# Moving dependent DMA issues from the SyncE queue to the GpSimd queue, and one weight split behind a normalisation, in a two-layer GDN / attention / FFN kernel

## The chip, the cores and the metric

One core of one Trainium2 chip runs the whole program. Time is device microseconds (us) of one execution; several executions are timed and their median is the kernel's time. One further execution is taken by the hardware profiler, and every trace row below is from that one. Engine names are those of the profile: PE is the matrix engine (PEld its weight loads), DVE, ACT and POOL are VectorE, ScalarE and GpSimd, SP is SyncE, which here only issues DMAs. A name with a q behind it (SPq, POOLq) is an engine's instruction queue; it runs its instructions in the order that the program gives them, so an issue that waits holds up every issue behind it.

## The reference

The reference computes a two-layer backbone on 256 latent tokens and 256 context tokens of width 2048, all in float32. Layer 0 is a mixer of 8 bidirectional gated-DeltaNet heads (a chunked linear recurrence that needs the inverse of a triangular matrix for every chunk, head and direction) beside 8 neighbourhood-attention heads; layer 1 is a gated short convolution. Each layer is modulated by factors computed from a conditioning vector and is followed by a SwiGLU FFN of hidden width 5632. In short:

```
for l in range(2):
    shifts, scales, gates = split(silu(c) @ ada_w[l] + ada_b[l])
    h = rmsnorm(x) * g * (1 + scale) + shift
    y = even_mixer(h, hc, ...) if l == 0 else shortconv_mixer(h, ...)
    x = x + gate1 * y
    x = x + gate2 * swiglu(rmsnorm(x) * g' * (1 + scale') + shift')
return rmsnorm(x)
# inside even_mixer, per head, direction and chunk of 64 tokens:
t_inv = inverse(eye + strict_lower(kb @ k.T * decay))
u, w  = t_inv @ (v * beta), t_inv @ (kb * exp(gc))
S     = S * exp(g_last) + k_dec.T @ (u - w @ S)
```

## The kernel before, in words

**Weights.** Every matrix product streams its weight from HBM in pieces of 128 x 1024 (`raw`, 512 KB, loaded on SP's queue by `load_w`, line 235). `split_w` makes two parts of each piece, a rounded `whi` (ACT, line 175) and a remainder `wlo` (DVE, line 249), and three matmuls (activation high by `whi`, high by `wlo`, low by `whi`) stand for one float32 product. `fm_stream` (line 347) holds the weight still, `tm_stream` (lines 302, 303, 307 and, for the last group, 319) holds the activation still. In layer 0's mixer there are four `raw` buffers and three of each split; later six of each.

**The order of the work.** The code only emits instructions. A scheduler at build time orders them per engine, by readiness on its own timeline and by the order of emission; `issue_after(i)` queues an instruction behind `i` on `i`'s engine (and only there), `follow` does so for one pair. While the projections stream, a plan keyed by stream steps (`P_CH`, `P_INV`) emits the stages of the GDN part, so that they interleave with the projections; `ada_mixer` adds the loads (`araw`, line 435) and sums (`acc`, line 441) of the modulation factors.

**The GDN stages.** `chunk_matrices(seq)` runs for the context (seq 1) and then for the latents (seq 0, `own_chunks`). For each group of four heads (q) and each token tile it makes the matrices `nt` (DVE, line 994), whose diagonal 32 x 32 blocks go to `dgs`, whose 32-wide off-diagonal blocks go to `n32` (POOL copies, line 1013) and whose 64-wide ones go to `n64`; `n64` and `n32` are stored to DRAM (lines 1020 and 1021, shown as `nd<-n`), the diagonal blocks go out to `dl` and come back as `lsol` (lines 1023, 1027), are inverted by substitution on DVE (lines 1036 and 1038) and stored as `dz` (line 1045). `load_diag` clears `xd` and `xdT` (POOL, lines 1060 and 1061) and reads `dz` back with 8 DMAs (line 1066) per sequence and q: 32 rows by 16 blocks by 32 floats each. There are two buffers of `xdT` and one of each `xd`. `inverses` (matmuls at lines 1092, 1099, 1105) builds the whole inverse from them, and `scan` runs the recurrence over it. `scan` loads keys as `ktok` and values as `vtok` (`load_tok`, line 956); for seq 1 and q 1 the keys go to the buffer of `lsol`, the source of one of the `dz` stores. All of these DMAs are issued by SP. POOL issues seven DMAs of its own, the reload `hC<-h_d` (line 1284).

**Evacuation of the value projection.** `stage` copies a finished PSUM bank to one of three buffers `nst` (`copy`, lines 170 and 172, in turn on ACT and DVE) and SP stores it (line 1260, `kb_d<-nst` and `vb_d<-nst`).

**Normed streams.** Three streams begin right behind a residual sum and take its RMSNorm as input: the gate projection of the FFN of layer 0, the convolution's input projection, and the gate projection of the FFN of layer 1. `Lead.scale` normalises the first 512 columns of the first token tile on DVE (line 1427, kept as `xi`) behind the sum of squares (line 1418) and `rstd` (lines 218 to 223, of which the square root, line 219, is on ACT); `Lead.turn` transposes them on PE. `Norm.step` modulates and splits them (ACT line 1473, DVE lines 1475 and 1482), and keeps its last ACT and DVE instructions as `behind`. `w_steps` queues the split of pieces HEAD-1, HEAD and HEAD+1 (3, 4 and 5) behind those; piece 2 (HEAD-2) has no such order. The first four pieces make the first group of matmuls.

Of the kernel before, what the change touches and what calls it, by code (L numbers as in the profile page):

```python
# [55 lines left out]
HEAD = 4  # L56
# [55 lines left out]
def body(tc, x, c, ctx, c_ctx, ada_w, ada_b, norm_mix, norm_ffn, ffn_w_gate, ffn_w_up, ffn_w_down,  # L112
# [3 lines left out]
    PE, ACT, DVE, POOL, SP = nc.tensor, nc.scalar, nc.vector, nc.gpsimd, nc.sync  # L116
# [112 lines left out]
    def load_w(segs, k0, nk):  # L229
        W = sum(s[2] for s in segs)  # L230
        raw = wp["pool"].tile([128, nk, W], F32, name="raw", tag="raw", bufs=wp["raw"])
        o = 0
        for ap, c0, w in segs:
            with tc.high_priority() if urgent[0] else Stack():
                SP.dma_start(raw[:, :, o:o + w], ap.rearrange("(k p) n -> p k n", p=128)[:, k0:k0 + nk, c0:c0 + w])
            o += w
        return raw.rearrange("p k n -> p (k n)")
# [3 lines left out]
    def split_w(raw, behind=None):  # L241

        hi = wp["pool"].tile([128, 1024], F32R, name="whi", tag="whi", bufs=wp["split"])
        lo = wp["pool"].tile([128, 1024], F32R, name="wlo", tag="wlo", bufs=wp["split"])
        with Stack() as order:
            for ins in behind or ():
                order.enter_context(tc.issue_after(ins.ins))
            acopy(hi, raw)
            last_lo[0] = DVE.tensor_tensor(lo, raw, hi, op=OP.subtract).ins  # L249
        return hi, lo  # L250

    def w_steps(segs, ks, behind=None, first=None):

        W = sum(s[2] for s in segs)
        nk = 1024 // W
        for g in range(0, len(ks), nk):
            assert ks[g + nk - 1] == ks[g] + nk - 1
            hi, lo = first if first and not g else split_w(load_w(segs, ks[g], nk), behind.behind if behind and g // nk in (HEAD - 1, HEAD, HEAD + 1) else None)
            for j in range(nk):
                yield ks[g] + j, hi[:, j * W:(j + 1) * W], lo[:, j * W:(j + 1) * W]  # L260

# [301 lines left out]
    p = smt()  # L563
# [20 lines left out]
    ks = list(range(KT))  # L584
# [93 lines left out]
    kd = dram.tile([128, 4, 8, 128], F32, name="kd")  # L678
# [5 lines left out]
    def hslice(d_, t0, n, q):  # L684
        return d_[:, t0:t0 + n, q * 4:q * 4 + 4, :].rearrange("p t h e -> p t (h e)")
# [125 lines left out]
    for b in range(8):  # L811
# [4 lines left out]
        p = smt()  # L816
# [134 lines left out]
        ACT.activation(em, pD.rearrange("p (i e) -> p i e", i=4), AF.Exp)  # L951
        return em

    def load_tok(tag, d_, t0, q, room=None):
        t = (g4(tag, tag) if room is None else room).rearrange("p (t h e) -> p t h e", t=2, h=4)
        SP.dma_start(t.rearrange("p t h e -> p t (h e)"), hslice(d_, t0, 2, q))
        return t

    def load_feat(tag, src, pool_=None, bufs=1):
# [4 lines left out]
    def chunk_matrices(seq):  # L964


        t0 = 2 * seq
        if seq:
            n64 = gw.tile([128, 16, 64], F32, name="n64", tag="n64", bufs=1)
            n32 = gw.tile([128, 16, 32], F32, name="n32", tag="n32", bufs=1)  # L970
            dgs = g4("dgs", "diag")
        else:
            n64 = lgo.tile([128, 1024], F32, name="n64", tag="o_t", bufs=2).rearrange("p (n c) -> p n c", n=16)
            n32 = g4("n32", "vtok")[:, 0:512].rearrange("p (n c) -> p n c", n=16)
            dgs = lgo.tile([128, 1024], F32, name="dgs", tag="o_t", bufs=2)
        dgs = dgs.rearrange("p (n c) -> p n c", n=32)
        for q in range(2):
            ktok = load_tok("ktok", kd, t0, q)
# [6 lines left out]
            for ti in range(2):  # L985
# [25 lines left out]
                for j in range(4):  # L1011
                    d, i = j % 2, j ^ 1
# [4 lines left out]
        lsol = g4("lsol", "lsol").rearrange("p (r c) -> p r c", r=32)  # L1017
        nd64 = dram.tile([128, 16, 64], F32, name="nd64", tag="nd64", bufs=2)
        nd32 = dram.tile([128, 16, 32], F32, name="nd32", tag="nd32", bufs=2)
        SP.dma_start(nd64, n64)  # L1020
        SP.dma_start(nd32, n32)
        dl = dram.tile([4, 32, 32, 32], F32, name="dl", tag="dl", bufs=2)
        SP.dma_start(dl.rearrange("b r n c -> (b r) n c"), dgs)
        for b in range(4):
# [16 lines left out]
        dz = dram.tile([2, 4, 2, 2, 8, 1024], F32, name="dz", tag="dz", bufs=2)  # L1041
# [14 lines left out]
    def load_diag(dz, q, tag="diag"):  # L1056

        xd = g4("xd", tag).rearrange("p (n c) -> p n c", n=16)
        xdT = gw.tile([128, 16, 128], F32, name="xdT", tag="xdT", bufs=XDT)
        POOL.memset(xd, 0.0)  # L1060
        POOL.memset(xdT, 0.0)
        for b in range(4):
            s_ = slice(b * 32, b * 32 + 32)
            c_ = slice((b % 2) * 32, (b % 2) * 32 + 32)
            for v, m_ in ((0, xd[s_, :, c_]), (1, xdT[s_, :, s_])):
                SP.dma_start(m_, dz[v, b, q].rearrange("d t (r c) -> r (d t) c", r=32))
        return xd, xdT

    def inverses(off, diag, q):
# [42 lines left out]
    def scan(q, seq, xdT, AT=None, qT=None, kT=None, o_t=None):  # L1112

        hs = [q * 4 + i for i in range(4)]
        if kT is None:
            kT = load_feat("kT", kTd[:, seq, q * 4:q * 4 + 4, :])
        ktok = load_tok("lsol" if seq and q else "ktok", kd, 2 * seq, q)
        vtok = load_tok("vtok", vd_, 2 * seq, q, lgo.tile([128, 1024], F32, name="vtok1", tag="o_t", bufs=2) if seq and q else None)
        visited = set()
        for step in range(2):  # L1120
            for d in range(2):
                ti = step if d == 0 else 1 - step
                tt = 2 * seq + ti
                tok = slice(ti * 128, ti * 128 + 128)
                zero = seq and step == 0
                sv = state[:, d, q * 4:q * 4 + 4, :]
                if not zero:
                    pP = gdt()
                    for i in range(4):
                        PE.matmul(pP[:, i * 128:(i + 1) * 128], kT[:, i, tok], sv[:, i, :], start=True, stop=True)  # L1130
                    R = g2("R")
                    for i in range(4):
                        DVE.scalar_tensor_tensor(R[:, i, :], pP[:, i * 128:(i + 1) * 128],
                                                 negegc[:, d, tt, hs[i]:hs[i] + 1], vtok[:, ti, i, :],
                                                 op0=OP.mult, op1=OP.add)
                if not seq:
                    pQ = gdt()
                    for i in range(4):
                        PE.matmul(pQ[:, i * 128:(i + 1) * 128], qT[:, i, tok], sv[:, i, :], start=True, stop=True)
                    for i in range(4):  # L1140
                        o = o_t[:, ti, i, :]
                        e = eg[:, 0, d, tt, hs[i]:hs[i] + 1]
                        if tt in visited:
                            DVE.scalar_tensor_tensor(o, pQ[:, i * 128:(i + 1) * 128], e, o, op0=OP.mult, op1=OP.add)
                        else:
                            ACT.activation(o, pQ[:, i * 128:(i + 1) * 128], AF.Copy, scale=e)
                pY = gdt()
                for i in range(4):
                    rhs = vtok[:, ti, i, :] if zero else R[:, i, :]
                    PE.matmul(pY[:, i * 128:(i + 1) * 128], xdT[:, d * 8 + ti * 4 + i, :], rhs, start=True, stop=True)  # L1150
                if seq or step == 0:
                    vd = g2("vd")
                    for i in range(4):
                        ACT.activation(vd[:, i, :], pY[:, i * 128:(i + 1) * 128], AF.Copy,
                                       scale=brest[:, d, tt, hs[i]:hs[i] + 1])
                    pS = gdt()
                    for i in range(4):
                        PE.matmul(pS[:, i * 128:(i + 1) * 128], ktok[:, ti, i, :], vd[:, i, :], start=True, stop=True)
                    if zero:
                        acopy(sv, pS.rearrange("p (i e) -> p i e", i=4))  # L1160
                    else:
                        for i in range(4):
                            DVE.scalar_tensor_tensor(sv[:, i, :], sv[:, i, :], eg[:, 2, d, tt, hs[i]:hs[i] + 1],
                                                     pS[:, i * 128:(i + 1) * 128], op0=OP.mult, op1=OP.add)
                if not seq:
                    vn = g2("vn")
                    for i in range(4):
                        ACT.activation(vn[:, i, :], pY[:, i * 128:(i + 1) * 128], AF.Copy,
                                       scale=beta[:, d, tt, hs[i]:hs[i] + 1])
                    pA = gdt()  # L1170
                    for i in range(4):
                        PE.matmul(pA[:, i * 128:(i + 1) * 128], AT[:, d * 8 + ti * 4 + i, :], vn[:, i, :], start=True, stop=True)
                    ov = o_t[:, ti]
                    DVE.tensor_tensor(ov, ov, pA.rearrange("p (i e) -> p i e", i=4), op=OP.add)
                visited.add(tt)
# [197 lines left out]
    held = na_scores(0)  # L1373
    for h in range(8):
# [4 lines left out]
        held = ahead  # L1379
# [255 lines left out]
    first = begin(tm_stream([(od_w_in[0], D, 1024)], ks, lhs1, [0, 1], ce, Norm(leads.pop(), dhi, dlo, scc[1, 0], shc[1, 0])))  # L1635
# [6 lines left out]
    for half in range(2):  # L1642
# [8 lines left out]
        for f in range(8):  # L1651
            k = half * 8 + f
            p = smt()
# [64 lines left out]
```

## Time and profile before

| | us |
|---|---|
| median of 3 timed runs | 2697.98 (2696.09 to 2699.02) |
| the profiled execution | 2700.74 |
| its span, from the first to the last instruction | 2698.6 |
| DVE busy | 1915.9 |
| ACT busy | 1274.9 |
| POOL busy | 47.8 |

A timeline or chain row begins with its start in us from the start of the span and its length; then come the engine, the line, and output <- input of the instruction. In square brackets stand the idle time ahead of it and what ended that. A row of windows has the stretch, then for each engine its busy time with the number of instructions, then the granted PE clock (1 is full), the busy share of the DMA engines and GB/s. Matmul ends are modelled: adjacent full matmuls start 0.23 us apart though each is given 0.39 us. A row of waits has the waiting instruction, what it waited for, the total in us, how often, and the longest.

### The profile page before, as it was taken

How to read it: one execution, taken by the hardware profiler on the slowest of the kernel's cores; microseconds unless marked ns; L12 is line 12 of the kernel's file. 1: busy time of each engine (PE TensorE's matmuls, PEld its weight loads, DVE VectorE, ACT ScalarE, POOL GpSimd, SP SyncE). 2: the span in 40 equal slices, each digit the busy share in tenths (PEclk: the TensorE clock that was granted, in tenths of full speed). 3: DMA queues.
4: the chain of work that ended last, by engine and by line, in shares of the span. 5: the costliest groups of instructions: out<-in, count | busy, mean ns of one | idle time of the engine just before them, and what ended most of it. 6: DMA issues, size and time to landing. Idle time of an engine off the chain costs nothing.

```text
span 2698.6 us, 37488 instructions
## 1 busy us (share of the span) xinstructions
PE 2646.0 (98%) x13775; PEld 2183.0 (81%) x13775; DVE 1915.9 (71%) x2645; ACT 1274.9 (47%) x1848; POOL 47.8 (2%) x73
## 2 busy tenths in 40 slices
PE   6999999999999999999999999999999999999998
PEld 4688888888887888888888878888788888888886
DVE  3378798866698866776788878898565655545665
ACT  3258633235455444444455564444454444445554
POOL 0000101010000000000000000000000000000000
PEclk8999999999999999999999999999999999999999
DMA  9945588996496988888887859997576777666653
GB/s 368 357 150 172 182 267 262 295 306 188 158 348 239 330 290 293 291 288 291 277 294 261 298 180 331 334 338 255 167 254 220 238 228 237 209 202 212 194 195 110
DMA packets 280027, 682.02 MB, mean 253 GB/s; under 512 B 50813, under 2 KB 93461, under 8 KB 278435
## 3 DMA queue, kind: packets, MB, share of 16 engines
q1 hardware_dynamic: 273516, 666.46, 73.5%
q10 hardware_dynamic: 4423, 9.50, 1.0%
q0 software_dynamic: 1904, 3.67, 0.4%
q8 instruction: 108, 1.77, 0.3%
q14 instruction: 76, 0.62, 0.1%
HBM read 657.48 MB, written 22.05 MB: 252 GB/s over the span
## 4 chain that ended last, share of the span: by engine, by line
PE 90%; DVE 3%; DMA 3%; ACT 1%; SPq 1%; issue 1%; DVEq 0%; ACTq 0%
PE mm L302 21%; PE mm L307 21%; PE mm L303 21%; PE mm L347 10%; PE mm L319 8%; PE sm L194 2%; PE sm L605 1%; PE gd L347 1%; DMA araw<-in_ada_w_dram 1%; DMA dz<-lsol 1%; DVE acc L441 1%; PE sm L1328 0%; PE gd L949 0%; DMA xn<-in_ctx_dram 0%; DVE wlo L249 0%
## 5 line engine op out<-in xcount | busy, mean ns | idle before, releaser
L249 DVE TENSOR_TENSOR wlo<-raw,whi 128x1024 fp32r<-128x1024 f32 x800 | 971.9, 1222 | 458.6 <-ACT whi L175 450.0
L175 ACT ACTIVATE whi<-raw 128x1024 fp32r<-128x1024 f32 x800 | 843.9, 1062 | 844.1 <-PE mm L307 627.8
L302 PE MATMUL mm<-whi,fhi 128*128 128x512 f32 x1232 | 482.0, 393 | 2.6 <-DVE fhi L1475 2.6
L303 PE MATMUL mm<-wlo,fhi 128*128 128x512 f32 x1232 | 479.7, 390 | 0.5 <-DVE wlo L249 0.5
L307 PE MATMUL mm<-whi,flo 128*128 128x512 f32 x1232 | 389.9, 390 | 0.0
L407 DVE SCALAR_TENSOR_TENSOR acc<-araw,cT,acc 128x1024 f32<-128x1024 f32 x224 | 286.7, 1280 | 39.8 <-DMA araw<-in_ada_w_dram 36.9
L302 PEld LDWEIGHTS mm<-whi,fhi 128*128 128x128 f32 x1232 | 231.3, 188 | 50.9 <-DVE fhi L1475 4.0
L307 PEld LDWEIGHTS mm<-whi,flo 128*128 128x128 f32 x1232 | 231.1, 188 | 48.4
L303 PEld LDWEIGHTS mm<-wlo,fhi 128*128 128x128 f32 x1232 | 231.2, 188 | 47.7 <-DVE wlo L249 1.2
L302 PE MATMUL mm<-whi,ahi 128*128 128x512 f32 x664 | 259.0, 390 | 0.0
L303 PE MATMUL mm<-wlo,ahi 128*128 128x512 f32 x664 | 258.3, 389 | 0.0
L347 PE MATMUL mm<-hB,whi 128*128 128x512 f32 (+1 forms) x840 | 234.6, 366 | 1.0 <-DVE hB L629 1.0
L307 PE MATMUL mm<-whi,alo 128*128 128x512 f32 x664 | 206.6, 389 | 0.0
L347 PEld LDWEIGHTS mm<-hB,whi 128*128 128x128 f32 x840 | 147.7, 189 | 24.5 <-DVE hB L629 2.3
L178 ACT ACTIVATE ahi<-prodT 128x256 fp32r<-128x256 f32 x176 | 73.0, 418 | 182.9 <-PE mm L303 178.0
L347 PE MATMUL mm<-hB,wlo 128*128 128x512 f32 (+1 forms) x420 | 149.7, 365 | 0.0
L307 PEld LDWEIGHTS mm<-whi,alo 128*128 128x128 f32 x664 | 124.6, 188 | 26.0
L302 PEld LDWEIGHTS mm<-whi,ahi 128*128 128x128 f32 x664 | 124.7, 188 | 25.7
L303 PEld LDWEIGHTS mm<-wlo,ahi 128*128 128x128 f32 x664 | 124.6, 188 | 25.6
L441 DVE SCALAR_TENSOR_TENSOR acc<-araw,cT,acc 128x512 f32<-128x512 f32 x180 | 133.9, 746 | 2.9 <-DMA araw<-in_ada_w_dram 2.3
L302 PE MATMUL mm<-whi,dhi 128*128 128x512 f32 x336 | 131.1, 392 | 1.2 <-DVE dhi L1475 1.2
L303 PE MATMUL mm<-wlo,dhi 128*128 128x512 f32 x336 | 130.7, 390 | 0.0
(412 smaller groups left out, 3523.3 us busy)
## 6 DMA issues: line engine op xcount, KB each, us to landing
araw<-in_ada_w_dram SPq DMA_DIRECT2D x288, 512.0 KB, 5.3
raw<-in_ffn_w_down_dram SPq DMA_DIRECT2D x176, 512.0 KB, 4.7
raw<-in_ffn_w_gate_dram SPq DMA_DIRECT2D x160, 512.0 KB, 4.4
raw<-in_ffn_w_up_dram SPq DMA_DIRECT2D x160, 512.0 KB, 4.7
raw<-in_ev_w_in_dram SPq DMA_DIRECT2D x112, 512.0 KB, 4.2
araw<-in_ada_w_dram SPq DMA_DIRECT2D x192, 256.0 KB, 5.1
raw<-in_od_w_in_dram SPq DMA_DIRECT2D x96, 512.0 KB, 5.1
raw<-in_ev_w_out_dram SPq DMA_DIRECT2D x32, 512.0 KB, 7.0
```

Source lines behind the costliest of these rows:

```text
L175: ACT.activation(dst, src, AF.Copy)
L178: ACT.activation(hi, src, AF.Copy)
L194: return PE.transpose(dst, src, ident[:n, :n])
L249: last_lo[0] = DVE.tensor_tensor(lo, raw, hi, op=OP.subtract).ins
L302: PE.matmul(ps[ti][n], a, hi[:, n * 512:(n + 1) * 512], start=first, stop=False)
L303: ins = PE.matmul(ps[ti][n], a, lo[:, n * 512:(n + 1) * 512], start=False, stop=False).ins
L307: last_mm[0] = PE.matmul(ps[ti][n], b, hi[:, n * 512:(n + 1) * 512], start=False, stop=False).ins
L319: ins = PE.matmul(ps[ti][n], a(t), w[:, c_], start=False, stop=a is ll and hi is group[-1][0]).ins
L347: last_mm[0] = PE.matmul(o, wt, h_(slice(0, len(ws)), mv, k), start=i == 0 and g == 0 and j == 0, stop=i == len(ks) - 1 and g == len(group ...
L407: DVE.scalar_tensor_tensor(acc, raw, cT[:, k:k + 1], acc, op0=OP.mult, op1=OP.add)
L441: DVE.scalar_tensor_tensor(accs[n], raws.pop(i), cT[:, k:k + 1], accs[n], op0=OP.mult, op1=OP.add)
L605: ins = PE.matmul(pr[32 * j:32 * j + 32, :], cT2[:, g + j, :], raw[:, j].rearrange("p s n -> p (s n)"), start=g == 0, stop=g == KT - 4).ins
```

## The change

Four edits. The store of the 32-wide blocks (`nd32`, twice) is issued by POOL instead of SP. The 32 loads of the diagonal blocks in `load_diag` are issued by POOL. The keys of seq 1 and q 1, which go to the buffer of `lsol`, are loaded by POOL. And in a normed stream the split of piece HEAD-2 (the third) is put behind `Lead`'s first scaling `xi`; that instruction is on DVE, so the order holds for `wlo` alone and not for `whi`.

```diff
@@ w_steps
-            hi, lo = first if first and not g else split_w(load_w(segs, ks[g], nk), behind.behind if behind and g // nk in (HEAD - 1, HEAD, HEAD + 1) else None)
+            held = None
+            if behind and g // nk in (HEAD - 1, HEAD, HEAD + 1):
+                held = behind.behind
+            elif behind and g // nk == HEAD - 2:
+                held = [behind.lead.xi]
+            hi, lo = first if first and not g else split_w(load_w(segs, ks[g], nk), held)
@@ load_tok
-    def load_tok(tag, d_, t0, q, room=None):
+    def load_tok(tag, d_, t0, q, room=None, queue=SP):
         t = (g4(tag, tag) if room is None else room).rearrange("p (t h e) -> p t h e", t=2, h=4)
-        SP.dma_start(t.rearrange("p t h e -> p t (h e)"), hslice(d_, t0, 2, q))
+        queue.dma_start(t.rearrange("p t h e -> p t (h e)"), hslice(d_, t0, 2, q))
@@ chunk_matrices
         SP.dma_start(nd64, n64)
-        SP.dma_start(nd32, n32)
+        POOL.dma_start(nd32, n32)
@@ load_diag
             for v, m_ in ((0, xd[s_, :, c_]), (1, xdT[s_, :, s_])):
-                SP.dma_start(m_, dz[v, b, q].rearrange("d t (r c) -> r (d t) c", r=32))
+                POOL.dma_start(m_, dz[v, b, q].rearrange("d t (r c) -> r (d t) c", r=32))
@@ scan
-        ktok = load_tok("lsol" if seq and q else "ktok", kd, 2 * seq, q)
+        ktok = load_tok("lsol", kd, 2 * seq, q, queue=POOL) if seq and q else load_tok("ktok", kd, 2 * seq, q)
```

## The prediction, made before any run of the changed kernel

> **What bounds the kernel now.** I read the page first, then the windows, then the waits and the timelines of the places where PE is idle.
>
> ```profile
> span 2698.6 us, 37488 instructions
> ...
> PE 2646.0 (98%) x13775; PEld 2183.0 (81%) x13775; DVE 1915.9 (71%) x2645; ACT 1274.9 (47%) x1848; POOL 47.8 (2%) x73
> ```
>
> PE is the bound: it is idle for 2698.6 - 2646.0 = 52.6 us of the span. No edit here takes a matmul away, so all that the change can win is idle time of PE and time at a lower clock. What it can lose has no such cap. The profiled execution took 2700.74 us, 2.76 us over the median of 2697.98; I make the sum against 2700.74 and take the same difference off the median.
>
> Windows of 50 us say where PE is not full, and windows of 5 us what its clock does behind a gap:
>
> ```profile
> 450.00:500.00 50.00, 50.00 (x433) 41.57 (x432) 38.29 (x80) 16.20 (x29) 4.89 (x10) 1.00 0.84 279
> 550.00:600.00 50.00, 46.58 (x352) 44.47 (x351) 29.31 (x53) 19.98 (x42) 3.32 (x3) 0.97 0.97 304
> 800.00:850.00 50.00, 47.16 (x210) 38.78 (x209) 43.74 (x68) 20.36 (x32) 0.00 (x0) 0.97 0.77 274
> 565.00:570.00 5.00, 2.63 (x16) 2.63 (x17) 2.36 (x4) 1.69 (x2) 0.39 (x1) 0.83 0.79 208
> 570.00:575.00 5.00, 5.00 (x38) 5.00 (x38) 4.26 (x8) 1.93 (x6) 0.00 (x0) 0.82 0.99 304
> 845.00:850.00 5.00, 4.61 (x16) 3.61 (x17) 2.68 (x11) 3.06 (x7) 0.00 (x0) 0.68 0.22 90
> ```
>
> Two stretches that the edits touch lose time: 3.42 us of idle in 550 to 600 and 2.84 us in 800 to 850. Behind each gap the granted clock drops. Behind the first it costs 5 x 0.17 + 5 x 0.18 = 1.75 us of matmul time, behind the second 5 x 0.32 = 1.6 us. From 450 to 500 PE is full.
>
> **The DMA edits: what stalls PE near 565 us.** PE's row, the DVE copy that it waits for, and SP's queue ahead of that:
>
> ```profile
> 567.37 0.51 PE L347 MATMUL mm<-hA,whi 128*128 128x256 f32 x2 [3.42 <-DVE nst L172]
> 566.62 0.69 DVE L172 COPY nst<-mm 128x512 f32<-128x512 f32 x1 [6.10 <-DMA vb_d<-nst]
> 554.32 0.60 ACT L170 ACTIVATE nst<-mm 128x512 f32<-128x512 f32 x1 [1.34 <-PE mm L319]
> 543.57 13.35 DMA dz<-lsol
> 547.64 0.33 SPq L435 DMA_DIRECT2D araw<-in_ada_w_dram  x1
> 557.00 0.38 SPq L956 DMA_DIRECT2D lsol<-kd  x1
> 558.47 2.05 SPq L1066 DMA_DIRECT2D xd<-dz  x3
> 561.15 5.45 DMA vb_d<-nst
> SPq L956 <- DMA dz<-lsol: 8.9, 1, 8.9
> ```
>
> The chain reads backwards. PE needs a PSUM bank; the copy that empties it needs an `nst` buffer; all three are full from 554.9 (ACT's third copy) and wait for their stores; the first store is issued only at 561.15 and lands 5.45 us later. It was late because SP stood 8.9 us at the load of the second keys into `lsol`, which must not start before the `dz` store out of `lsol` has landed (543.57 + 13.35 = 556.92), and then issued four `xd` loads.
>
> Those loads leave SP. Behind the `araw` issue at 547.64 SP is then free for a weight piece and the `vb_d` stores. The last `nst` copy ends at 554.92; a store issued then and as slow as the quoted one lands at about 560.4, more than 3 us ahead of the moment when PE ran dry (567.37 - 3.42 = 563.95). So I take the whole idle time and its clock: 3.42 + 1.75 = 5.2 us. It can't be more at this place; it is nothing if transfers and not SP's order are what is late (second rival).
>
> What the waiting loads now hold up is POOL. Behind them on POOL stand its own clears of `xd` and `xdT`, and in the first part of the mixer the `n32` copies; DVE waits for those before it overwrites `nt`. POOL is busy for 47.8 us of 2698.6, so its compute covers nothing of note, and its order is what matters.
>
> The `nd32` store stands at another wait:
>
> ```profile
> SPq L1021 <- POOL n L1013: 5.9, 1, 5.9
> ```
>
> SP loses 5.9 us there, but PE is full in the window around it (450 to 500, above): the weight buffers hide it. The next store, of the 64-wide blocks, waits for copies of the same `nt`, so SP stays held almost as long. I take nothing, with 0 to 0.5 us either way.
>
> **What POOL's queue costs.** The trace has seven loads on it:
>
> ```profile
> 529.28 2.26 POOL L1284 DMA_DIRECT2D hC<-h_d  x3 [2.21 <-PE mm L307]
> 538.73 0.72 POOL L1284 DMA_DIRECT2D hC<-h_d  x1 [7.19 <-issue]
> q0 software_dynamic: 1904, 3.67, 0.4%
> hC<-h_d POOLq DMA_DIRECT2D x7, 512.0 KB, 10.1
> xd<-dz SPq DMA_DIRECT2D x16, 64.0 KB, 3.0
> ```
>
> Seven loads make 1904 packets, 272 each, or 17 on each of 16 DMA engines. Three go out at once; the fourth stands 7.19 us at nothing that the profile names, until about when the first must have landed (529.28 + 10.1 = 539.4). I read this as a queue that holds at least 51 and fewer than 68 packets per engine. A diagonal load moves 64 KB in rows of 32 floats, 512 pieces, so 32 per engine and, by the same count, one more: 33. Two are 66. So I expect one diagonal load at a time, each at the pace of its landing. Bounds for one: 0.7 us (the issue alone) and 10.1 us (an `hC` load, eight times the bytes). I take 3.0 + 0.7 = 3.7 us, the landing of the same load from SP plus POOL's issue, because that row is of the same bytes.
>
> The Trainium skill (DMA: Bandwidth & Descriptors, "Anatomy of one DMA — SWDGE (gpsimd) path") gives about 2.0 us plus the bytes at 436 GB/s for a GpSimd DMA. By it one load is an estimated 2.15 us and four are 8.6 us; the 10.1 us of the `hC` row is far above its 3.2 us for 512 KB, so I lean on the row.
>
> Where are four such loads due? The tightest place is the second context inverse:
>
> ```profile
> 501.28 0.96 POOL L1060 MEMSET xd<- 128x1024 f32 x1 [23.23 <-PE gd L1092]
> 504.93 2.35 SPq L1066 DMA_DIRECT2D xd<-dz  x4
> 510.54 0.24 PE L1092 MATMUL gd<-xd,n 32*32 32x32 f32 x2
> 604.60 0.75 PE L1092 MATMUL gd<-xd,n 32*32 32x32 f32 x64
> ```
>
> Cleared at 502.24, loaded by SP from 504.93, used at 510.54. From POOL the loads start 2.7 us earlier but take 4 x 3.7 = 14.8 us: they are there at 517.0, 6.5 us later than now. The order on PE is not given by hand here. The build's scheduler sees that the loads come later and puts projection matmuls ahead, so only what the chip takes beyond the scheduler's notion comes out as a stall. The bounds are 0 and 6.5 us; I take 1 us, since PE has streams ready to put ahead.
>
> The other diagonal loads have more room. The first set belongs to the stage planned at step 2 of the streams and is used by the one at step 16 (`P_CH`, `P_INV`): I expect no wait. The latents' first inverse begins at 604.60, 47.7 us behind the landing of `dz` (556.92); its eight loads take 29.6 us at 3.7.
>
> **The split behind the scaling.** The first normed stream:
>
> ```profile
> 840.70 0.74 DVE L441 SCALAR_TENSOR_TENSOR acc<-araw,cT,acc 128x512 f32<-128x512 f32 x1
> 842.13 1.23 DVE L249 TENSOR_TENSOR wlo<-raw,whi 128x1024 fp32r<-128x1024 f32 x1 [0.68 <-ACT whi L175]
> 843.34 0.73 DVE L441 SCALAR_TENSOR_TENSOR acc<-araw,cT,acc 128x512 f32<-128x512 f32 x1
> 844.57 0.49 DVE L1427 TENSOR_SCALAR rtmp<-xs,nx0r 128x512 f32<-128x512 f32 x1
> 842.00 0.19 ACT L219 ACTIVATE nx0s<-nx0v 128x1 f32<-128x1 f32 x1
> 844.13 1.26 PE L450 MATMUL sm<-cs,acc 128*128 128x1 f32 x8 [2.45 <-DVE acc L441]
> 849.05 0.50 PE L302 MATMUL mm<-whi,fhi 128*128 128x512 f32 x1 [0.39 <-DVE fhi L1475]
> ```
>
> DVE waits 0.68 us for `whi` and spends 1.23 us on the third piece's `wlo`, while the square root is done at 842.19 and PE waits for the `acc` behind. The second normed stream has no such split there:
>
> ```profile
> 1582.89 0.20 ACT L219 ACTIVATE nx0s<-nx0v 128x1 f32<-128x1 f32 x1 [0.41 <-DVE nx0v L218]
> 1583.90 0.49 DVE L1427 TENSOR_SCALAR rtmp<-xs,nx0r 128x512 f32<-128x512 f32 x1
> 1584.91 1.22 DVE L249 TENSOR_TENSOR wlo<-raw,whi 128x1024 fp32r<-128x1024 f32 x1
> 1586.92 0.50 PE L302 MATMUL mm<-whi,dhi 128*128 128x512 f32 x1 [0.37 <-DVE dhi L1475]
> ```
>
> From the root to the scaling it takes 1.01 us, and from the scaling to the first matmul 3.02 us. With the split moved, the first stream can do the same: `acc` fits ahead of the root's end, the scaling starts at 842.00 + 1.01 = 843.01, the first matmul at 846.03. That is 849.05 - 846.03 = 3.0 us. The low bound leaves the half clock in place: the first stream's own 844.57 to 849.05, 4.48 us, gives 847.49 and 1.6 us. I take 2.8. In the second stream the split already stands behind the scaling (1584.91 after 1583.90), so the edit does nothing; the third is built alike, and I take nothing for it.
>
> **The sum.** -5.2 (stall at 565) - 2.8 (first normed stream) + 1.0 (late diagonal blocks) = -7.0 us: 2700.74 becomes 2693.7, and the median 2697.98 becomes 2691.0.
>
> **The rivals.**
> *Slower: the diagonal loads go out one by one, and PE stands at an inverse.* If one takes 6 us under load, between 3.7 and 10.1, the four at 502.24 end at 526.2, 15.7 us behind the old use, and the latents' sets bunch up likewise. For it: the 7.19 us row, and DMA engines 0.97 busy from 550 to 600. Against: the scheduler can move the inverse back. Priced at 15.7 plus a dropped clock (1.75) less 8.0: +9.5 us, a median of 2707.4. The net turns at a loss of 8 us, which is (510.54 - 502.24 + 8.0) / 4 = 4.1 us per load if the order on PE stays.
>
> *About the same: the transfers are late, not SP.* The DMA engines are 0.97 busy around the stall; stores and weights that are issued earlier may land no earlier. Then only the normed stream gains, 2.8 us: 2695.2. Against it: the wait for `nst` ended with a store that had not been issued for over 6 us.
>
> The Trainium skill says the like (DMA: Bandwidth & Descriptors, "Issuing engines are not separate DMA queues"): issuing from more engines saves only issue time. The 8.9 us wait on SP is not issue time, so I hold the row against the rule.
>
> **How the numbers follow.** My case 0.50; about the same 0.27; slower 0.23. About 0.2%, 5.4 us, is what a measurement of this kernel can tell from no change. My case alone runs from 2688.2 (5.2 + 3.0 us, and the 1.6 us of the second gap's clock on top, nothing lost at the diagonal blocks) to 2692.6. The range starts 2.2 us lower, for the scatter of the runs (2696.09 to 2699.02), at 2686, and reaches to 2708, just past the slower rival's price. That leaves out the worse half of that rival, 0.12, and some 0.05 below.
>
> **What would show it.** Right: no PE row near 565 with an idle of over 1 us, granted clock 1.00 from 550 to 600 and from 845 to 850; SP's 8.9 us wait gone; the DVE scaling within 1.1 us of the square root in the first normed stream. Wrong: POOL rows of line 1066 more than 5 us apart with PE idle ahead of line 1092 or 1099; DVE idle ahead of line 994 because `n32` copies stand behind POOL's loads; or the same `nst` wait with its store issued early.

## The result, and the profile after

The changed kernel takes 2735.28 us (median of 4 runs, 2731.74 to 2738.34) against 2698.31 us for the kernel before: a ratio of 1.0143, 95% interval 1.0131 to 1.0155. It is 37 us slower. The forecast was 2691.0 us, with a range up to 2708. The profiled execution took 2738.01 us, its span is 2736.2 us. Lines below 256 have kept their numbers; line 994 of before is now 999, 1013 is 1018, 1066 is 1071, 1092 is 1097, 1099 is 1104.

PE's line of the page:

```profile
PE 2651.1 (97%) x13775; PEld 2188.2 (80%) x13775; DVE 1917.6 (70%) x2645; ACT 1274.4 (47%) x1848; POOL 70.4 (3%) x108
```

PE is now idle for 2736.2 - 2651.1 = 85.1 us where it was 52.6, so 32.5 us more; the same matmuls take 5.1 us more, at a lower clock (0.989 on the mean of the span, where it was 0.994). That is the whole 37.6 us between the spans. Windows of 50 us say where:

```profile
400.00:450.00 50.00, 31.66 (x158) 26.06 (x156) 23.11 (x42) 8.50 (x13) 8.17 (x12) 0.87 0.54 177
450.00:500.00 50.00, 44.92 (x292) 38.46 (x292) 42.05 (x82) 17.26 (x32) 9.46 (x20) 0.89 0.66 217
550.00:600.00 50.00, 50.00 (x384) 44.35 (x373) 35.10 (x73) 18.58 (x36) 7.90 (x11) 1.00 0.95 310
```

The stretch of the old stall, 550 to 600, is full at clock 1.00, and nowhere between 400 and 700 does PE wait for `nst`. The new loss begins between 400 and 500, where PE had been all but full. POOL's own timeline of that stretch (start, length, instruction, in brackets the idle time ahead):

```profile
412.50 0.68 POOL L1071 DMA_DIRECT2D xdT<-dz  x1 [0.79 <-DMA dz<-lsol]
417.83 0.66 POOL L1071 DMA_DIRECT2D xdT<-dz  x1 [4.66 <-issue]
...
438.01 0.65 POOL L1071 DMA_DIRECT2D xdT<-dz  x1 [1.85 <-issue]
440.48 0.66 POOL L1071 DMA_DIRECT2D xdT<-dz  x1 [1.82 <-issue]
...
450.86 0.66 POOL L1071 DMA_DIRECT2D xd<-dz  x1 [1.92 <-issue]
451.56 1.27 POOL L1018 COPY n<-nt 32x128 f32<-32x128 f32 x4
```

Twelve diagonal loads, the eight of the context's first set and the four `xdT` of its second, go out one at a time: (450.86 - 412.50) / 11 = 3.49 us apart, at best 2.47 us. Each but the first stands at "issue" before it goes out, that is at nothing that the profile names. Only then does POOL reach the `n32` copies. What stood behind these copies, DVE's row and then PE's:

```profile
452.86 2.16 DVE L999 SCALAR_TENSOR_TENSOR nt<-gd,beta,em 128x128 f32<-128x128 f32 x8 [23.07 <-POOL n L1018]
455.08 1.11 PE L194 MATMUL gd<-cs,ktok 128*128 128x128 f32 x4 [22.39 <-DVE nt L999]
```

`nt` has one buffer. DVE may not write the next one until POOL has copied the last one's blocks out, and PE's next matmul in program order needs a bank that DVE empties. So PE stood for 22.39 us because of loads that nobody needed yet: the context's first inverse starts at 495.80, 40 us later. The waits of 395 to 760 us show the rest (total, times, longest):

```profile
DVE nt L999 <- POOL n L1018: 23.1, 1, 23.1
PE gd L1097 <- DMA xd<-dz: 7.5, 3, 2.9
PE gd L1104 <- DMA xdT<-dz: 4.9, 1, 4.9
```

22.4 + 7.5 + 4.9 = 34.8 us of new idle time on PE, less the 3.4 us of the old stall, is 31.4 of the 32.5.

The first normed stream, DVE, ACT and PE rows in order of time:

```profile
876.73 0.16 DVE L1423 TENSOR_REDUCE ss<-ssx 128x1 f32<-128x4 f32 x1 [0.19 <-ACT jk L1415]
878.29 0.18 ACT L219 ACTIVATE nx0s<-nx0v 128x1 f32<-128x1 f32 x1
879.29 0.49 DVE L1432 TENSOR_SCALAR rtmp<-xs,nx0r 128x512 f32<-128x512 f32 x1
880.29 1.22 DVE L249 TENSOR_TENSOR wlo<-raw,whi 128x1024 fp32r<-128x1024 f32 x1
884.17 0.48 PE L307 MATMUL mm<-whi,fhi 128*128 128x512 f32 x1
```

The scaling stands 1.00 us behind the square root and the split behind the scaling, as intended. From the sum of squares to the scaling it is 2.56 us. But the clock of PE falls here as it did before:

```profile
880.00:885.00 5.00, 5.00 (x22) 4.28 (x23) 4.55 (x11) 3.06 (x7) 0.00 (x0) 0.66 0.34 105
```

### The profile page after: what moved, and what is told of

It is laid out like the page before. It is cut to its first block, busy times and chain, and to the rows that moved or that the text cites. A ratio compares the mean times of both kernels' runs of the same rounds, so it can differ in the third digit from the quotient of the medians.

```text
span 2736.2 us, 37514 instructions
## 1 busy us (share of the span) xinstructions
PE 2651.1 (97%) x13775; PEld 2188.2 (80%) x13775; DVE 1917.6 (70%) x2645; ACT 1274.4 (47%) x1848; POOL 70.4 (3%) x108
## 3 DMA queue, kind: packets, MB, share of 16 engines
q0 software_dynamic: 3232, 6.82, 0.8%
## 4 chain that ended last, share of the span: by engine, by line
PE 82%; issue 5%; DMA 5%; DVE 4%; ACT 1%; POOL 1%; SPq 0%; ACTq 0%; DVEq 0%; POOLq 0%
PE mm L307 19%; PE mm L312 19%; PE mm L308 19%; PE mm L352 10%; PE mm L324 7%; DMA araw<-in_ada_w_dram 3%; PE sm L194 2%; DVE acc L412 1%; PE sm L610 1%; DVE wlo L249 1%; PE gd L352 1%; DMA dz<-lsol 1%; PE gd L954 0%; DMA cs<-in_cst_dram 0%; ACT whi L175 0%
```

## The experiments

All times are medians beside runs of the kernel before on the same chip, with the recorded ratio and its 95% interval; that ratio differs a little from the quotient of the two medians. The theory after the result: POOL's queue has room for one diagonal load, twelve of them stand ahead of the `n32` copies, and DVE and PE wait behind the copies; a smaller part is lost at the inverses. Its rivals: the waits at the inverses are the real bound and the wait at `nt` only comes first; the path moves such small pieces slowly however many loads fit; or the other parts of the change cost as well.

**1. The diagonal loads back on SP**, the rest of the change kept.

```diff
-                POOL.dma_start(m_, dz[v, b, q]...)
+                SP.dma_start(m_, dz[v, b, q]...)
```

> The changed kernel with the diagonal blocks' loads back on SP; the second keys and nd32 stay on POOL, the split stays held. Theory (the diagonal loads on POOL are the loss: 12 of them, 3.49 us apart, stand ahead of the n32 copies on POOL, so that DVE waits 23.1 us at line 999): the wait is gone, POOL's copies run within 2 us of DVE's solve, and the time falls below before, 2690 to 2696 us. Rival (whatever else is on POOL, or the new order of the queues, costs as well): 2700 us or more, with PE idle in front of a tile other than these. Second rival (the keys on POOL save nothing by themselves): 2696 to 2700 us.

Measured: 2703.36 us, 1.0019 (1.0009 to 1.0028). The 23 us wait is gone, so the loss is the diagonal loads', but the time stays 5 us above before: the first rival has a point. Something else in the change costs (runs 5 to 7).

**2. The diagonal loads on POOL alone**, in the kernel before.

```diff
-                SP.dma_start(m_, dz[v, b, q]...)
+                POOL.dma_start(m_, dz[v, b, q]...)
```

> The kernel before with one edit alone: the diagonal blocks' loads on POOL. Theory: the same 12 loads in a row between 412 and 451 us and the same DVE wait of 22 to 24 us at the nt line; the time is 2733 to 2745 us, that is, the whole loss of the change or a few us more since the two other parts gain. Rival (the loss comes from the parts together, such as keys and diagonal blocks in one queue): below 2720 us.

Measured: 2733.02 us, 1.0122 (1.0106 to 1.0139). This one edit has nearly the whole loss, and the same wait:

```profile
453.66 1.12 PE L194 MATMUL gd<-cs,ktok 128*128 128x128 f32 x4 [20.77 <-DVE nt L994]
```

**3. Each diagonal load cut in two.** Of the changed kernel:

```diff
-                POOL.dma_start(m_, dz[v, b, q].rearrange("d t (r c) -> r (d t) c", r=32))
+                for d in range(2):
+                    POOL.dma_start(m_[:, d * 8:d * 8 + 8], dz[v, b, q, d].rearrange("t (r c) -> r t c", r=32))
```

> The changed kernel with each diagonal load cut in two by direction, 256 packets each in place of 512. The hC loads of the kernel before, 272 packets each, went three at a time. Theory (POOL's queue has room for three such halves and for only one whole load, and what a whole load costs is mostly the time from its issue to its landing): the 24 halves start 1.0 to 1.4 us apart, the stretch shrinks from 38 to 25 to 32 us, the DVE wait from 23.1 to 10 to 17 us, and the time is 2718 to 2730 us. Rival (the queue moves its packets at a fixed rate, some 7 ns each): halves 1.75 us apart, the stretch stays near 40 us, and the time is 2734 us or more.

Measured: 2693.11 us, 0.9980 (0.9971 to 0.9989), better than theory and rival, and faster than the kernel before by just what can be told. POOL's timeline:

```profile
414.62 1.75 POOL L1072 DMA_DIRECT2D xdT<-dz  x3
420.26 1.80 POOL L1072 DMA_DIRECT2D xdT<-dz  x3 [3.89 <-issue]
...
433.25 0.58 POOL L1072 DMA_DIRECT2D xd<-dz  x1 [1.46 <-issue]
433.87 1.27 POOL L1018 COPY n<-nt 32x128 f32<-32x128 f32 x4
```

The halves (256 pieces each) go three at a time, as the `hC` loads did. 14 of them start within 18.63 us, 1.43 us apart, or 2.87 us per whole load. But the build also put the copies behind 14 halves (seven loads) in place of twelve loads. Pace and order changed together, so the run doesn't tell room from rate; run 14 does.

**4. The `n32` copies on ACT**, whole loads on POOL.

```diff
-                    POOL.tensor_copy(n32[...], nt[...])
+                    acopy(n32[...], nt[...])
```

> The changed kernel with the n32 copies on ACT in place of POOL: POOL's loads stay in their order and one at a time, but nothing of DVE or PE waits for a POOL instruction behind them. Theory (two thirds of the loss is that link): the 23 us wait of nt for n32 is gone, PE runs through 430 to 455 us, what stays is the waits at the inverses (535 to 539 us and 646 to 656 us, some 15 us with the clock that they cost), and the time is 2700 to 2714 us. Rival (the late diagonal blocks bound the mixer, and the wait at nt only comes first): PE waits as long for xd at a later place, and the time is 2725 us or more.

Measured: 2712.62 us, 1.0056 (1.0040 to 1.0072), as the theory had it. With the link gone 37 us of loss become 15, give or take what the new build order is worth. Most of what is left stands at the inverses, where PE waits 10.2 us in this trace for loads that still go one by one; two of these waits:

```profile
521.45 0.25 PE L1097 MATMUL gd<-xd,n 32*32 32x32 f32 x4 [1.91 <-DMA xd<-dz]
525.23 1.06 PE L1097 MATMUL gd<-xd,n 32*32 32x32 f32 x58 [2.86 <-DMA xd<-dz]
```

**5. The split alone**, in the kernel before.

```diff
+            elif behind and g // nk == HEAD - 2:
+                held = [behind.lead.xi]
```

> The kernel before with one edit alone: the split of the third piece behind the first scaling. The kernel with the diagonal loads back on SP came out 5 us slower than before (2703.36 against 2697.57 us), so one of its three parts costs. Theory (the split does what the prediction said, and no more than PE's wait there allows): the sum of squares stands 2.5 to 2.6 us ahead of the scaling in place of 4.13, PE's first gate matmul 1 to 2 us earlier, and the time is 2695 to 2698 us. Rival (the split is the part that costs, in one of the two other normed streams or by a new order): 2700 us or more.

Measured: 2695.14 us, 0.9991 (0.9982 to 1.0000): 2.4 us less, with nothing at the upper end of the interval. ACT's root, DVE's scaling and PE's first gate matmul:

```profile
839.50 0.18 ACT L219 ACTIVATE nx0s<-nx0v 128x1 f32<-128x1 f32 x1
840.50 0.49 DVE L1432 TENSOR_SCALAR rtmp<-xs,nx0r 128x512 f32<-128x512 f32 x1
845.38 0.47 PE L307 MATMUL mm<-whi,fhi 128*128 128x512 f32 x1
```

**6. The second keys alone** on POOL.

```diff
-        ktok = load_tok("lsol" if seq and q else "ktok", kd, 2 * seq, q)
+        ktok = load_tok("lsol", kd, 2 * seq, q, queue=POOL) if seq and q else load_tok("ktok", kd, 2 * seq, q)
```

> The kernel before with one edit alone: the second keys' load on POOL. Theory (SP stood behind that load, and the value projection's stores behind it): the stall of PE at 564 us (3.7 us) is gone and the time is 2692 to 2695 us. Rival (the diagonal loads, issued by an SP that doesn't stand, go out earlier and collide with the weights, or the build puts PE's work in another order): another stall of 3 to 6 us appears in the mixer and the time is 2698 to 2704 us.

Measured: 2696.56 us, 1.0000 (0.9991 to 1.0009): neither. But for one diagonal load that moves up by one place on SP, every other instruction of the program keeps its place here, so the run is clean. SP's queue, then PE:

```profile
543.86 0.33 SPq L435 DMA_DIRECT2D araw<-in_ada_w_dram  x1
552.73 0.86 SPq L1066 DMA_DIRECT2D xd<-dz  x2
...
556.14 1.37 SPq L1260 DMA_DIRECT2D vb_d<-nst  x3
562.16 0.51 PE L347 MATMUL mm<-hA,whi 128*128 128x256 f32 x2 [1.46 <-DVE nst L172]
```

SP still stands from 544.19 to 552.73, now at the first diagonal load, which waits for the same `dz`. PE's stall is 1.46 us where it was 3.42, and the median shows none of it. The stall is no fixed size, though. Up to the first normed stream run 5 is the same program as the kernel before, with keys and loads on SP, and at this matmul (line 352 there) it has

```profile
564.04 0.50 PE L352 MATMUL mm<-hA,whi 128*128 128x256 f32 x2 [1.03 <-DVE nst L172]
```

Run 11, with the keys on POOL, has 2.23 us there. What the keys take off the stall can't be told from these executions.

**7. The store of the 32-wide blocks alone** on POOL.

```diff
-        SP.dma_start(nd32, n32)
+        POOL.dma_start(nd32, n32)
```

> The kernel before with one edit alone: the store of the 32-wide blocks on POOL. Theory (free): within 2 us of before. Rival (this is the part of the changed kernel that costs the 5 us which the diagonal loads don't explain): 2701 us or more.

Measured: 2703.27 us, 1.0022 (1.0013 to 1.0031): the rival. Not POOL pays, though. With this one issue moved the build ordered everything anew: set side by side, 1955 of PE's 12589 matmuls stand at another place (in the control, run 6, none, and in run 5, 14). A wait of SP's and a PE row between 700 and 760 us, where the kernel before has neither:

```profile
SPq L435 <- DVE acc L443: 27.9, 1, 27.9
749.52 2.08 PE L302 MATMUL mm<-whi,yhi 128*128 128x512 f32 x4 [2.57 <-ACT whi L175]
```

SP stands 27.9 us at an `araw` load with the output projection's weights behind it, and PE waits for the first of these. Run 1 has the same stall, 2.56 us ahead of 751.06. Its order on PE differs from run 7's in 14 places only, so its 5 us and these are most likely the same. That the new order and not the move makes them isn't shown: the two came together.

**8. The copies on ACT and the loads halved**: the diffs of runs 3 and 4 together.

> The kernel with the n32 copies on ACT (2712.62 us) and, besides, each diagonal load cut in two. Here no engine's order lets DVE wait for a POOL load, so what changes is the pace of the loads alone. Theory (a load of 512 packets has the queue for itself, three of 256 share it): halves start 1.4 us apart on the mean, the latest diagonal blocks come 10 us or more earlier, PE's waits at the inverses (2.3, 2.3, 3.3 and 5.6 us) are gone but for 3 us in all, and the time is 2692 to 2700 us. Rival (the pace is the same by bytes and packets, and the gain of the halves came only from another order on POOL): 2708 us or more.

Measured: 2703.31 us, 1.0024 (1.0014 to 1.0034), between the two. Against run 4 the time is 9 us less, and PE waits for no diagonal block any more. A new wait, of another build order, stands in the way of the rest:

```profile
776.01 1.84 PE L455 MATMUL sm<-cs,acc 128*128 128x1 f32 x8 [6.26 <-DVE acc L446]
```

**9. Halved loads on SP**, in the kernel before, as a control.

```diff
-                SP.dma_start(m_, dz[v, b, q]...)
+                for d in range(2):
+                    SP.dma_start(m_[:, d * 8:d * 8 + 8], dz[v, b, q, d]...)
```

> The kernel before with each diagonal load cut in two, all still on SP: a control. The changed kernel with halves on POOL was 4.5 us faster than before. Theory (halves help on POOL only, where a whole load has the queue for itself; SP's loads of the kernel before follow each other 0.5 us apart already): 32 more issues of 0.4 to 0.5 us each on SP, no gain, 2697 to 2704 us. Rival (half loads land earlier wherever they are issued): 2694 us or less.

Measured: 2698.44 us, 1.0004 (0.9992 to 1.0016). Halves don't help as such; they help on POOL.

**10. Run 3 with `nd32` back on SP.**

```diff
-        POOL.dma_start(nd32, n32)
+        SP.dma_start(nd32, n32)
```

> The changed kernel with halved diagonal loads, and nd32 back on SP. Alone, moving nd32 cost 5 us, and its trace shows the cause as a new build order on SP (two araw loads that wait 28 us stand ahead of the output projection's weights). Theory (the cost belongs to the order that was built, not to the move; with halves and nd32 on POOL no such stall at 747 us was there): no 5 us to be had, 2690 to 2697 us. Rival (nd32 on POOL costs 5 us in itself): 2687 to 2689 us.

Measured: 2697.19 us, 0.9994 (0.9985 to 1.0004): the rival is out, and the time is 0.2 us above the theory's band. Taking back an edit that cost 5 us by itself made run 3 no faster, so the edit has no fixed price. But the build order changed here too, so this run doesn't separate the order from the move either.

**11. Keys and split together**, in the kernel before: the diffs of runs 5 and 6.

> The kernel before with the two parts that cost nothing: second keys on POOL and the held split. Theory (the split's 2.4 us, the keys' nothing, since SP stands behind the first diagonal load in their place): 2694 to 2697 us. Rival (the prediction's terms add up once each stall has only one cause): 2690 to 2692 us.

Measured: 2695.70 us, 0.9996 (0.9987 to 1.0005), the theory's.

**12. Whole loads on POOL, queued behind the `n32` copies.** Of the changed kernel:

```diff
+        with tc.issue_after(last_n32[0].ins):
+            diag = load_diag(parts[2], 0)
```

and the same for the second set.

> The changed kernel, whole loads on POOL, with one order added: the context's two sets of diagonal loads are queued behind the last n32 copy of the latents. Theory (half of the loss is the link, and half the pace): DVE's 23 us wait for n32 is gone; the first set now starts near 472 us at 3.5 to 5 us a load, is needed at 493 to 505 us and is 5 to 15 us late there, and the clears of dgs behind six of the loads delay DVE's substitution; in all 2710 to 2725 us. Rival (order alone was wrong, the pace is hidden): 2695 to 2705 us.

Measured: 2734.07 us, 1.0140 (1.0123 to 1.0157): slower than theory and rival said, as slow as the changed kernel. The wait at `nt` is gone, and this stands in its place, on DVE and on PE:

```profile
493.76 1.06 PE L1098 MATMUL gd<-xd,n 32*32 32x32 f32 x58 [5.98 <-DMA xd<-dz]
514.34 0.20 DVE L1042 TENSOR_TENSOR sub_tmp<-lsol,dgs 128x31 f32<-128x31 f32 x1 [27.32 <-POOL dgs L1037]
521.42 0.77 PE L308 MATMUL mm<-whi,hA 128*128 128x512 f32 x1 [14.47 <-DVE nst L172]
```

The next POOL instructions in the queue are the clears of `dgs`. They now stand behind the loads, DVE's substitution stands 27.32 us behind the clears, and a copy that PE needs behind that. I had named this and priced it far too low. Here the order only chose who pays.

**13 and 14. The room of POOL's queue.** The program gives POOL's DMA queue a memory of 1024 (an argument where the program is made). Doubling that needs space, taken from one of six `araw` buffers; run 13 is the control with five buffers and 1024.

```diff
-AB = 6
+AB = 5
-    nc = _bacc.Bacc(..., dynamic_dma_scratch_size=1024)
+    nc = _bacc.Bacc(..., dynamic_dma_scratch_size=2048)
```

Both programs have the same instructions in the same order on every engine.

> The changed kernel with five araw buffers in place of six: the control for the next run, whose larger queue memory needs the space. Both theories: near the changed kernel, 2728 to 2745 us, whole loads one at a time, DVE waiting about 20 us at the nt line for n32.

> The same program as the control, instruction for instruction on every engine, but with the memory that the program gives POOL's DMA queue doubled from 1024 to 2048. Theory (room: at 1024 the queue holds at least 51 and fewer than 68 packets per DMA engine, so one load of 33; doubled it holds 102 to 135, so three of 33, or four at the upper end): the first three or four loads issue 0.7 us apart, the 12 loads take 14 to 25 us in place of 38, DVE's wait for n32 falls from about 20 to under 8 us, and the time is 2695 to 2712 us. Rival (the pace is the rate at which POOL or its queue moves 128-byte packets, or the source's latency): the loads stay 2.5 us or more apart from the first on, and the time stays within 4 us of the control.

Measured: the control 2739.63 us, 1.0146 (1.0128 to 1.0163); with 2048, 2701.68 us, 1.0009 (0.9999 to 1.0018). 38 us between them, from the size of a queue. POOL's timeline of the control, and the PE row that waits:

```profile
410.49 0.68 POOL L1071 DMA_DIRECT2D xdT<-dz  x1 [0.79 <-DMA dz<-lsol]
417.02 0.66 POOL L1071 DMA_DIRECT2D xdT<-dz  x1 [5.85 <-issue]
...
447.17 0.66 POOL L1071 DMA_DIRECT2D xd<-dz  x1 [1.83 <-issue]
451.39 1.12 PE L194 MATMUL gd<-cs,ktok 128*128 128x128 f32 x4 [21.99 <-DVE nt L999]
```

and the same of the larger queue:

```profile
411.37 1.96 POOL L1071 DMA_DIRECT2D xdT<-dz  x3 [1.13 <-DMA dz<-lsol]
417.34 0.66 POOL L1071 DMA_DIRECT2D xdT<-dz  x1 [4.02 <-issue]
418.99 1.93 POOL L1071 DMA_DIRECT2D xdT<-dz  x3 [0.99 <-issue]
...
429.23 0.66 POOL L1071 DMA_DIRECT2D xd<-dz  x1 [2.52 <-issue]
429.94 1.27 POOL L1018 COPY n<-nt 32x128 f32<-32x128 f32 x4
433.45 1.12 PE L194 MATMUL gd<-cs,ktok 128*128 128x128 f32 x4 [3.33 <-DVE nt L999]
```

Three at once, then a stand until room is free: the twelve start within 17.9 us in place of 36.7, and PE's wait falls from 21.99 to 3.33 us. The seven `hC` loads, which went three and then one by one before, now go out in a row:

```profile
534.23 4.92 POOL L1289 DMA_DIRECT2D hC<-h_d  x7 [2.69 <-PE mm L312]
```

Only the queue's memory differs between runs 13 and 14, so its room is the cause of nearly the whole loss.

## Why the prediction was wrong

*The step that failed.* "The first set belongs to the stage planned at step 2 of the streams and is used by the one at step 16 (`P_CH`, `P_INV`): I expect no wait." I asked when these loads are needed, and not what stands behind them in POOL's queue meanwhile. I had written that the `n32` copies stand there, that DVE waits for them and that POOL's "order is what matters"; DVE idle behind these copies even stands among my signs of being wrong. Yet I put no price on it, neither in the sum nor in a rival. It was 22.4 us of idle PE and, by run 4, some 22 us of the 37. The rows were to be had in the profile of before, on POOL's timeline:

```profile
414.26 0.96 POOL L1060 MEMSET xd<- 128x1024 f32 x1 [39.92 <-DMA dz<-zsol]
418.50 0.61 POOL L1013 COPY n<-nt 32x128 f32<-32x128 f32 x2 [3.28 <-DVE nt L994]
...
435.75 0.62 POOL L1013 COPY n<-nt 32x128 f32<-32x128 f32 x2 [15.19 <-DVE nt L994]
```

`xd` is cleared and free to load just ahead of a group of copies, and the next group comes 17 us later. Eight loads at my own 3.7 us hold POOL for 29.6 us. Put ahead of the copies at 418.50 they end at 414.26 + 0.96 + 29.6 = 444.8. Until those copies are made DVE can't write the next `nt`, which before was ready for copying at 435.75. By my own numbers DVE was 9 us late at least.

*The reading of the queue was right, with a gap.* I expected one load at a time, from 17 packets per engine of an `hC` load and three of these at once. But two loads of 33 are 66, which is still below my bound of 68; that they went singly is what puts the room at 51 to 65. At twice the memory three of 33 (99) and seven of 17 (119) fit and four of 33 (132) don't, which agrees. What the count must be taken from is the pieces, though, and not the packets that the profile shows for a load on POOL (run 2, then run 3):

```profile
q0 software_dynamic: 2928, 5.77, 0.7%
q0 software_dynamic: 4256, 6.82, 0.8%
```

Against 1904 before, the 32 whole loads of run 2 add 1024, 32 each or two per engine. Run 3 has 1024 more than the 3232 of the changed kernel for 32 loads more: a half is 32 packets as well. Yet whole loads go singly and halves in threes.

I took 3.7 us a load, and the first twelve had 3.49. By the Trainium skill (DMA: Bandwidth & Descriptors, "Anatomy of one DMA — SWDGE (gpsimd) path") a load is an estimated 2.15 us; no gap between the starts of two loads in this trace is that short, the shortest being 2.47 us.

*The late diagonal blocks, +1.0 us.* Mis-sized: PE's waits for them are 7.5 + 4.9 = 12.4 us. At the second context inverse PE waits 2.33 and 2.26 us, inside my bounds of 0 and 6.5 but not the 1 us that I took on the ground that PE had streams to put ahead. For the latents I expected no wait from 29.6 us of loads in 47.7. PE waits there 2.9 and 4.9 us. These loads stand behind the second keys on POOL (8.59 us) and then go 4.9 us apart (16 loads from 584.69 to 658.75, with POOL's clears and two waits for PE among them), which is nearer to the 6 us of the slower rival than to 3.7.

*The stall at 565 us, -5.2 us.* PE's row is gone, and the clock is 1.00. The reason I gave was half of it: run 6 shows that behind the keys the first diagonal load waits for the same `dz`, so both have to leave SP; in the changed kernel no wait of SP for `dz` is left there. But the row is also missing in run 7, which leaves both on SP, and it is 1.03 us in run 5. I had taken one execution's wait for a fixed cost, so its absence doesn't show that the freed SP removed it. Run 14 moves both, has no wait for `nst` near 565, and gains nothing in all. The rule that other issuing engines save only issue time, which I held the row against (the Trainium skill, DMA: Bandwidth & Descriptors, "Issuing engines are not separate DMA queues"), agrees with these totals. In run 14 other waits of PE stand in the stall's place: 3.33 us for `nt`, 2.38 us at 590.51 for DVE, and 3.00 us at 846.78 for `acc`, where it was 2.45. In all PE is idle for 2704.0 - 2646.4 = 57.6 us in that execution, 5.0 more than before.

*The `nd32` store, 0 to 0.5 us.* It cost 5 us by itself (run 7), and nothing that run 10 could win back from run 3. I had counted the wait, and left out that the build orders PE, DVE, ACT and SP anew around a moved issue.

*The split, -2.8 us.* The mechanism was right: the scaling stands 1.00 us behind the root (1.01 forecast), and 2.56 us in place of 844.57 - 840.44 = 4.13 us behind the sum of squares, which stood before at

```profile
840.44 0.16 DVE L1418 TENSOR_REDUCE ss<-ssx 128x1 f32<-128x4 f32 x1 [0.19 <-ACT jk L1410]
```

The size was off. The first gate matmul comes 849.05 - 840.44 = 8.61 us behind the sum of squares before and 7.44 us after, a gain of 1.17 us, below even my low bound of 1.6 us. From the scaling to it are 4.88 us, not the 3.02 us of the second stream that I had taken over. The low bound had kept the low clock, and the low clock stayed: 0.66 from 880 to 885, where it had been 0.68 from 845 to 850. In time run 5 shows 2.4 us, with an interval from nothing to 4.9.

*The rivals.* The slower one had the right cause, loads one by one, and the wrong place: it priced the inverses at 15.7 + 1.75 = 17.5 us, where PE's waits there are 12.4 us, and missed the copies. Nothing of the prediction covered a loss of 37 us.

What stays open is the scatter of some 5 us between builds (runs 3 and 10 differ by 4 us in the direction opposite to run 7), and how much of it is the order of the instructions. Run 3 beats the kernel before by 0.2%; that its order will hold under another edit isn't shown.

## What to carry to other kernels

Before an issue moves to another engine's queue, list what stands behind it there until the queue has room again, and price that wait: when the data are needed says nothing about it. Count the pieces of a transfer (the stretches that lie together in memory, here rows of 32 floats) against the room of the queue; where one transfer fills it, cut the transfers smaller or give the queue more memory, since reordering alone (run 12) only changed who waits. In a program that a build orders by itself, moving one issue can give PE another order and a time 5 us off (run 7), so an experiment should say whether the order has stayed. And before a wait goes into a sum, see whether it has the same size in a second execution: the stall at 565 us had not.

## What the runs showed of the hardware

A GpSimd queue that is full holds the whole engine at "issue", compute behind it included: 23 us of DVE's waiting for a POOL that was busy for 3% of the span. The room goes with the memory given to it and with the pieces of a load: one load of 512 pieces at 1024, three at 2048, three of 256 pieces at 1024. The packets that the profile shows don't tell it: they are 32 for a load of 512 pieces and for one of 256.
